# Four instead of three of eight experts on 64 places, with unsplit float32 products

## The chip, the cores and the metric

The kernel runs on one core of one Trainium2 chip. The metric is the device time of one execution, in microseconds. It is the median of several executions, lower is better.

## The reference

The program is two layers of a hybrid encoder over 256 tokens of width 1024, all in float32. Each layer has an input projection, a convolution branch, a state-space branch, an output projection and a feed-forward part. The feed-forward part of the first layer is dense. That of the second layer is a mixture of eight experts, and each token goes to two of them:

```python
def swiglu(h, w_gate, w_up, w_down):
    return (jax.nn.silu(h @ w_gate) * (h @ w_up)) @ w_down

def top2_moe(h, router_w, router_b, w_gate, w_up, w_down):
    ...
    logits = (t @ router_w + router_b).astype(jnp.float32)
    top_val, top_idx = lax.top_k(logits, TOP_K)
    top_w = jax.nn.softmax(top_val, axis=-1)
    gates = jnp.sum(jax.nn.one_hot(top_idx, N_EXPERTS, dtype=jnp.float32)
                    * top_w[..., None], axis=1)
    out = jnp.zeros((bsz * seq_len, d), jnp.float32)
    for e in range(N_EXPERTS):
        out = out + gates[:, e:e + 1] * swiglu(t, w_gate[e], w_up[e], w_down[e]).astype(jnp.float32)
```

Here D_MODEL is 1024 and D_FF is 2816, so the three weight matrices of one expert hold 33 MiB, and those of eight experts 264 MiB. A final RMS norm gives the output. With the reference's inputs the router sends 58, 53, 93, 46, 60, 38, 73 and 91 tokens to experts 0 to 7.

## The kernel before

Everything but the experts stays as it is, so only the second layer's expert part (`moe`, and `route` inside it) is told here.

**Route.** `route` ranks the tokens of each expert and sorts the experts: place 0 is always expert 0, whose weights can be asked for before the routing is known, and places 1 to 7 hold the other seven by falling token count. The first `NL` places are the big ones, the last `NS` the small ones. A big expert has 128 token places (`CAP`), a small one 64 (`CAPS`). `route` also leaves a count (`cnt`) that tells whether any expert has more tokens than places. If so, `rest` at the very end computes what did not fit, with a loop over all experts; else `rest` is skipped.

**Blocks.** An expert's hidden width is cut into 11 blocks of 256 (`NB`). A block needs two transfers of 1 MiB from `m_gu` (gate and up weights) and one from `m_down`. The transfers are issued by SyncE in the order in which the blocks use them, into a ring of eight 1 MiB buffers (`NRA` = 6 and `NRB` = 2, both named `raw`), so each transfer waits until the buffer eight transfers before it is free.

**A big block** splits the weights: for each half of a buffer ScalarE writes the rounded part `wh` and VectorE the remainder `wl` (`split`, L93 and L75). This frees the buffer. TensorE then makes three products where one is meant (high by high, high by low, low by high): 24 matmuls of 512 columns into `acc`, a silu and a product on ScalarE and VectorE (`sl`), two transposes, a split of the activations (`mah`, `mal`), and 12 matmuls of 512 columns into `py`.

**A small block** uses `raw` unsplit, in float32. The 64 places are the stationary side, so two halves of the hidden width are put on the two 64-column halves of the array: 16 matmuls into `acc` (in the trace 32 records of 256 columns), one transpose (`sls`, `mas`), and 4 matmuls into `pys` (8 records). The buffer is free when TensorE is done with it.

**Order.** The blocks stand in one list. Four big blocks come first; then the small blocks are spread evenly over the remaining big ones:

```python
        seq, n0 = big[:4], len(big) - 4
        for i, v in enumerate(big[4:]):
            seq.append(v)
            seq += few[(i * len(few)) // n0:((i + 1) * len(few)) // n0]
```

In the loop over this list the first products of a block are followed by the second products of the block before it. TensorE, VectorE and ScalarE keep the program's order. During the first blocks, side work is mixed in (`side`): the token gathers `small` (all small experts at once) and `gather1` (places 1 and 2), and, from the first block of place 1 on, `gather3` (places 3 and 4). When an expert's last block is done, `back` (big) or `back_few` (small) scatters its result into `x`, the first half at once, the second half after the next block.

Of the kernel before, what the change touches and what calls it, by code (L numbers as in the profile page):

```python
# [19 lines left out]
T = 256  # L20
# [10 lines left out]
PAD = 384  # L31
SP = mybir.EngineType.SP
NRA, NRB, NHL = 6, 2, 4
NL, NS, CAPS = 5, 3, 64
# [24 lines left out]
class Body:  # L59
# [1129 lines left out]
    def route(self):  # L1189
# [114 lines left out]
        self.dr = self.dp.tile([128, NE, 3, 2], F32, name="dr")  # L1304
        rg = sp.tile([128, NE, 3, 2], F32, name="rg")
# [63 lines left out]
    def moe(self):  # L1369
# [50 lines left out]
        def alone():  # L1420

            t = [self.gtp.tile([128, 8, 128], F32R, name="x0", tag="gate") for _ in range(2)]
            for k2 in range(4):
                for src, dst in zip((self.hth, self.htl), t):
                    ps = self.misc()
                    for k in range(2):
                        kk = 2 * k2 + k
                        for b in range(2):
                            self.mm(ps[:, k * 256:(k + 1) * 256], src[:, b, kk * 128:(kk + 1) * 128],
                                    oh[:, b, 0:1].to_broadcast([128, 2, 128]), b == 0, b == 1)  # L1430
                    nc.scalar.copy(dst[:, 2 * k2:2 * k2 + 2], ps.rearrange("p (k s) -> p k s", k=2)[:, :, 0:128])
            tok[0] = [lambda k, t=t, i=i: t[i][:, k] for i in range(2)]
# [22 lines left out]

        def gather3():
            x = [self.gtp.tile([128, 4, 2, 128], F32R, name="x3", tag="gate") for _ in range(4)]
            both([lambda k, h=h: x[2 * h + k // 4][:, k % 4] for h in range(2)], 3)
            return pair(*(lambda k2, h=h: x[2 * h + k2 // 2][:, 2 * (k2 % 2):2 * (k2 % 2) + 2]
                          .rearrange("p k e s -> p (k e s)") for h in range(2)), 3)  # L1460
# [146 lines left out]
        alone()  # L1607
# [32 lines left out]
    def rest(self):  # L1640
# [3 lines left out]
        with tc.If(n > self.cap):  # L1644
            hf = [t.bitcast(F32) for t in (self.hth, self.htl)]
            with tc.For_i(0, NE, 1) as e:
                rg = self.gp.tile([128, 3, 2], F32, name="g_r")
                nc.sync.dma_start(rg, self.dr[:, bass.ds(e, 1)].rearrange("p o i b -> p (o i) b"))
                oh = self.gp.tile([128, 2, 128], F32, name="g_oh")
                for b in range(2):  # L1650
                    nc.vector.tensor_scalar(oh[:, b], self.iota, rg[:, 0, b:b + 1], None, op0=ALU.is_equal)
                oht = self.gp.tile([128, T], F32, name="g_oht")
                gs = self.gp.tile([128, 2], F32, name="g_gs")
                ps = self.misc()
                for b in range(2):
                    self.tr(ps[:, b * 128:(b + 1) * 128], oh[:, b])
                nc.scalar.copy(oht, ps[:, :T])
                ps = self.misc()
                for b in range(2):
                    self.mm(ps[:, 0:2], oh[:, b], rg[:, 1:3, b], b == 0, b == 1)  # L1660
                nc.vector.tensor_copy(gs, ps[:, 0:2])
                xg = self.gp.tile([128, 8, 128], F32, name="g_x")
                for k in range(8):
                    ps = self.misc()
                    for j in range(4):
                        i, b = divmod(j, 2)
                        self.mm(ps[:, :128], hf[i][:, b, k * 128:(k + 1) * 128], oh[:, b], j == 0, j == 3)
                    nc.scalar.copy(xg[:, k], ps[:, :128])
                py = self.psx.tile([128, D], F32, name="py")
                for b in range(NB):  # L1670
                    pg = self.acc()
                    w = self.gp.tile([128, 2, 4, 2, 256], F32, name="g_gu")
                    for i in range(2):
                        nc.sync.dma_start(w[:, i].rearrange("p k w f -> p (k w f)"),
                                          self.a["m_gu"][bass.ds(e, 1), b, i].rearrange("o p f -> p (o f)"))
                    for j in range(2):
                        for k in range(8):
                            self.mm(pg[:, 256 * j:256 * j + 256], xg[:, k], w[:, k // 4, k % 4, j], k == 0, k == 7)
                    sl = self.gp.tile([128, 256], F32, name="g_a")
                    nc.scalar.activation(sl, pg[:, :256], AF.Silu, scale=gs[:, 1:2])  # L1680
                    self.stt(sl, pg[:, 256:], gs[:, 1:2], sl, ALU.mult, ALU.mult)
                    ps = self.misc()
                    for i in range(2):
                        self.tr(ps[:, i * 128:(i + 1) * 128], sl[:, i * 128:(i + 1) * 128])
                    at = self.gp.tile([128, 2, 128], F32, name="g_at")
                    nc.scalar.copy(at.rearrange("p k s -> p (k s)"), ps[:, :256])
                    w = self.gp.tile([128, 2, D], F32, name="g_w")
                    nc.sync.dma_start(w.rearrange("p k f -> p (k f)"),
                                      self.a["m_down"][bass.ds(e, 1), b].rearrange("o p f -> p (o f)"))
                    for k in range(2):  # L1690
                        for h in range(2):
                            s = slice(512 * h, 512 * h + 512)
                            self.mm(py[:, s], at[:, k], w[:, k, s], b == 0 and k == 0, b == NB - 1 and k == 1)
                y = self.gp.tile([128, D], F32, name="g_y")
                nc.scalar.activation(y, py, AF.Copy, scale=gs[:, 0:1])
                for d in range(8):
                    ps = self.misc()
                    self.mm(ps[:, :T], y[:, d * 128:(d + 1) * 128], oht, True, True)
                    self.add(self.x[:, d], self.x[:, d], ps[:, :T])
# [236 lines left out]
```

## Time and profile before

| What | Value |
|---|---|
| Median of 3 executions | 1428.27 us (1427.89 to 1429.31) |
| The profiled execution's own time | 1430.8 us |
| Its span, first to last instruction | 1429.0 us |
| Mean granted TensorE clock, share of 2.4 GHz | 0.972 |
| First matmul of the first expert block | 681.87 us after the span's start |
| Last weight transfer issued | 1377 us |

All later rows are from that one profiled execution. In the rows, PE is TensorE's matmul side, PEld its weight load, DVE is VectorE, ACT is ScalarE and SP is SyncE. A matmul's duration includes its latency, so matmuls overlap, and the pace is read from one start to the next.

### The profile page before, as it was taken

What the parts mean: (1) busy time and instruction counts of PE and PEld (TensorE: products, weight loads), DVE (VectorE), ACT (ScalarE), POOL (GpSimd) and SP (SyncE); (2) the same over time, 40 slices, a digit from 0 to 9 for tenths busy, and PEclk for the clock granted to TensorE, in tenths of its full rate; (3) what the DMA queues carried; (4) which work ended last, traced back from release to release, by engine and by line L of the source; (5) the groups of instructions that cost most, each with busy time, mean ns of one, the idle gap of its engine ahead of it and who ended that gap; (6) DMA issues with size and microseconds to landing.
All of it is one profiled execution on the core that took longest, in us unless ns stands there. A gap on an engine that the chain in (4) does not pass through costs nothing. (4 is left out here: it accounts for less than half of the span.)

```text
span 1429.0 us, 23540 instructions
## 1 busy us (share of the span) xinstructions
PE 1341.0 (94%) x9291; PEld 1079.3 (76%) x9291; DVE 952.3 (67%) x1413; ACT 686.1 (48%) x968; POOL 84.3 (6%) x148
## 2 busy tenths in 40 slices
PE   6989989999998969888999999999999999999995
PEld 5868879999998858886876666667676676666663
DVE  7696675788885465765775665667666666666663
ACT  3432344454444524443675555555555555555551
POOL 1052220000120040000000000000000000000000
PEclk9999999999999989998999999999999999999996
DMA  5284444566678394564689999998999999999970
GB/s 218 97 258 150 168 133 150 191 220 207 221 234 285 132 299 130 180 222 159 236 313 362 394 347 407 405 417 338 405 421 419 365 418 351 414 368 416 409 301 31
DMA packets 78307, 399.73 MB, mean 280 GB/s; under 512 B 13024, under 2 KB 15728, under 8 KB 44400
## 3 DMA queue, kind: packets, MB, share of 16 engines
q1 hardware_dynamic: 65504, 371.22, 68.0%
q0 software_dynamic: 8448, 26.31, 5.7%
q8 instruction: 75, 1.23, 0.4%
q10 hardware_dynamic: 4240, 0.64, 0.3%
q14 instruction: 40, 0.33, 0.1%
HBM read 386.51 MB, written 11.62 MB: 279 GB/s over the span
## 5 line engine op out<-in xcount | busy, mean ns | idle before, releaser
L75 DVE TENSOR_TENSOR wl<-raw,wh 128x1024 fp32r<-128x1024 f32 x460 | 549.5, 1222 | 220.5 <-ACT wh L93 220.2
L93 ACT ACTIVATE wh<-raw 128x1024 fp32r<-128x1024 f32 x460 | 470.5, 1054 | 77.1 <-issue 35.8
L116 PE MATMUL acc<-wh,x 128*128 128x512 f32 x880 | 293.9, 401 | 0.0
L116 PEld LDWEIGHTS acc<-wh,x 128*128 128x128 f32 x880 | 165.5, 188 | 44.9 <-ACT wh L93 8.9
L116 PE MATMUL acc<-wl,x 128*128 128x512 f32 x440 | 173.0, 393 | 0.0
L116 PE MATMUL acc<-hf,wh 128*128 128x256 f32 x704 | 128.4, 285 | 0.0
L116 PE MATMUL acc<-raw,xs 128*64 128x256 f32 x1056 | 127.9, 384 | 0.0
L116 PE MATMUL acc<-hh,wh 128*128 128x256 f32 x352 | 105.1, 298 | 7.0 <-ACT hh L636 3.1
L116 PE MATMUL acc<-xg,raw 128*128 128x256 f32 x448 | 103.2, 388 | 6.8 <-DMA raw<-in_w_in 6.8
L116 PEld LDWEIGHTS acc<-hf,wh 128*128 128x128 f32 x704 | 109.0, 190 | 0.2
L116 PEld LDWEIGHTS acc<-raw,xs 128*64 128x64 f32 x1056 | 71.2, 137 | 46.9 <-issue 17.5
L116 PE MATMUL acc<-hh,wl 128*128 128x256 f32 x352 | 103.0, 293 | 1.7 <-DVE wl L75 1.7
L116 PE MATMUL acc<-hl,wh 128*128 128x256 f32 x352 | 102.9, 292 | 0.0
L116 PE MATMUL acc<-hf,wl 128*128 128x256 f32 x352 | 99.9, 284 | 2.0 <-DVE wl L75 2.0
L116 PEld LDWEIGHTS acc<-xg,raw 128*128 128x128 f32 x448 | 85.8, 195 | 19.1 <-ACT xg L682 6.8
L116 PEld LDWEIGHTS acc<-wl,x 128*128 128x128 f32 x440 | 83.1, 189 | 18.0 <-DVE wl L75 1.7
L116 PE MATMUL py<-wh,mah 128*128 128x512 f32 x220 | 89.6, 407 | 0.0
L116 PE MATMUL py<-wh,mal 128*128 128x512 f32 x220 | 86.1, 391 | 0.0
L116 PE MATMUL py<-wl,mah 128*128 128x512 f32 x220 | 86.0, 391 | 0.0
L1508 ACT ACTIVATE mah<-misc 128x256 fp32r<-128x256 f32 x55 | 21.1, 384 | 128.6 <-PE misc L124 128.3
L116 PEld LDWEIGHTS acc<-hh,wh 128*128 128x128 f32 x352 | 70.7, 201 | 10.8 <-issue 4.0
L75 DVE TENSOR_TENSOR mal<-misc,mah 128x256 fp32r<-128x256 f32 x55 | 23.3, 423 | 74.9 <-ACT mah L1508 74.8
(290 smaller groups left out, 2002.6 us busy)
## 6 DMA issues: line engine op xcount, KB each, us to landing
raw<-in_m_gu SPq DMA_DIRECT2D x176, 1024.0 KB, 8.0
raw<-in_m_down SPq DMA_DIRECT2D x88, 1024.0 KB, 8.3
raw<-in_w_in SPq DMA_DIRECT2D x56, 512.0 KB, 4.1
raw<-in_f_gate SPq DMA_DIRECT2D x22, 512.0 KB, 3.5
raw<-in_f_up SPq DMA_DIRECT2D x22, 512.0 KB, 3.7
raw<-in_f_down SPq DMA_DIRECT2D x22, 512.0 KB, 3.5
raw<-in_w_out SPq DMA_DIRECT2D x16, 512.0 KB, 3.5
hs<-hc POOLq DMA_DIRECT2D x32, 142.0 KB, 5.4
```

The source lines that it names most:

```text
L75: return self.nc.vector.tensor_tensor(out, a, b, op=op)
L93: self.nc.scalar.activation(h, raw, AF.Copy)
L116: return self.nc.tensor.matmul(out, l, r, start=start, stop=stop, **kw)
L1508: nc.scalar.activation(ah, pv, AF.Copy)
```

## The change

The numbers of places change from 5 big and 3 small to 4 and 4, so the expert with the fourth-smallest count (60 tokens with these inputs) moves from 128 places and split products to 64 places and unsplit ones. `gather3` is gone; `alone`, which gathered place 0, now also gathers place 3, as a piece of side work. A padding tile goes, and two small tiles of `route` move to another pool, to make room for the larger `xs`. The general path (`rest`) reads each expert's own count and skips the expert when it fits; its body moves to a function of its own, `rest_of`, unchanged.

```diff
-PAD = 384
+PAD = 0
...
-NL, NS, CAPS = 5, 3, 64
+NL, NS, CAPS = 4, 4, 64
...
-        pm = sp.tile([128, NE, NE], F32, name="pm")
+        pm = self.c2("pm", [128, NE, NE])
...
-        t8 = sp.tile([128, NE, NE], F32, name="t8")
+        t8 = self.c2("t8", [128, NE, NE])
...
-        self.dr = self.dp.tile([128, NE, 3, 2], F32, name="dr")
-        rg = sp.tile([128, NE, 3, 2], F32, name="rg")
+        self.dr = self.dp.tile([128, NE, 4, 2], F32, name="dr")
+        rg = sp.tile([128, NE, 4, 2], F32, name="rg")
...
+        self.add(few, few, ps[:, 16:24])
+        nc.vector.tensor_copy(rg[:, :, 3], few[:, :, None].to_broadcast([128, NE, 2]))
         nc.gpsimd.dma_start(self.dr, rg)
-        self.add(few, few, ps[:, 16:24])
...
-        def alone():
+        def alone(j):
...
+            tok[j] = [lambda k, i=i: t[i][:, k] for i in range(2)]
...
-                                    oh[:, b, 0:1].to_broadcast([128, 2, 128]), b == 0, b == 1)
+                                    oh[:, b, j:j + 1].to_broadcast([128, 2, 128]), b == 0, b == 1)
...
-        def gather3():
-            x = [self.gtp.tile([128, 4, 2, 128], F32R, name="x3", tag="gate") for _ in range(4)]
...
-        alone()
+        for _ in alone(0):
+            pass
...
                 if v == (1, 0):
-                    side.append(gather3())
+                    side.append(alone(3))
...
+                ne = self.gp.tile([1, 1], I32, name="g_n")
+                nc.vector.tensor_copy(ne, rg[0:1, 3, 0:1])
+                with tc.If(nc.values_load(ne[0:1, 0:1]) > self.cap):
+                    self.rest_of(e, rg, hf)
```

The instruction order shows what the list of blocks becomes. On ScalarE, in the middle of the expert part, a big block shows as an `sl` and a `mah` among its `wh` splits, a small one as an `sls` and a `mas`. Before, a stretch reads:

```order
L1492 ACTIVATE sls<-acc,gs_7641 128x128
L93 ACTIVATE wh<-raw 128x1024 x2
L1501 COPY mas<-misc 128x128
L93 ACTIVATE wh<-raw 128x1024 x3
L1492 ACTIVATE sl<-acc,gs_8180 128x256
L93 ACTIVATE wh<-raw 128x1024
L1508 ACTIVATE mah<-misc 128x256
L93 ACTIVATE wh<-raw 128x1024 x3
L1492 ACTIVATE sl<-acc,gs_8180 128x256
```

After the change a stretch of the same engine and part reads:

```order
L1488 ACTIVATE sls<-acc,gs_7643 128x128
L93 ACTIVATE wh<-raw 128x1024 x2
L1497 COPY mas<-misc 128x128
L93 ACTIVATE wh<-raw 128x1024
L1488 ACTIVATE sl<-acc,gs_8139 128x256
L93 ACTIVATE wh<-raw 128x1024
L1504 ACTIVATE mah<-misc 128x256
L93 ACTIVATE wh<-raw 128x1024 x2
L1488 ACTIVATE sls<-acc,gs_7643 128x128
```

Before, a small block (`sls`) is followed by one or by two big blocks (`sl`); after, a big block is always followed by a small one. In counts: of the blocks behind the first four, 51 big and 33 small become 40 big and 44 small. Before, each of the 33 small blocks stands alone between big ones, and 18 big blocks follow another big one. After, there are 40 pairs of a big and a small block and, four times, a second small block.

On TensorE, a small block before always stands behind a big one (`py` of the big block after the second `acc<-raw,xs`):

```order
L116 MATMUL pys<-raw,mas 64x512 x4
L116 MATMUL acc<-raw,xs 64x256 x8
L124 MATMUL misc<-ident,sl 128x128 x2
L116 MATMUL acc<-raw,xs 64x256 x8
L116 MATMUL py<-wh,mah 128x512
```

At one of the four places where two small blocks now stand together, TensorE's order is:

```order
L116 MATMUL py<-wh,mal 128x512
L116 MATMUL acc<-raw,xs 64x256 x8
L124 MATMUL misc<-ident,sls 128x128
L116 MATMUL acc<-raw,xs 64x256 x8
L116 MATMUL pys<-raw,mas 64x512 x4
L116 MATMUL acc<-wh,x_7383 128x512
```

The second small block has the transpose of a small block (`sls`) between its halves, and `pys` behind it instead of twelve `py`.

## Rows read from the trace of the kernel before

**Rows 1.** The page: busy time of TensorE; clock and bandwidth in 40 slices

```profile
PE 1341.0 (94%) x9291; PEld 1079.3 (76%) x9291; DVE 952.3 (67%) x1413; ACT 686.1 (48%) x968; POOL 84.3 (6%) x148
...
PEclk9999999999999989998999999999999999999996
...
GB/s 218 97 258 150 168 133 150 191 220 207 221 234 285 132 299 130 180 222 159 236 313 362 394 347 407 405 417 338 405 421 419 365 418 351 414 368 416 409 301 31
```

**Rows 2.** Stretches of the expert part: length, busy time, granted clock, DMA share, GB/s

```profile
682.00:740.00 58.00, 57.73 (x279) 48.25 (x278) 42.34 (x58) 39.30 (x54) 0.57 (x1) 1.00 0.73 275
...
1000.00:1100.00 100.00, 100.00 (x517) 68.88 (x517) 65.36 (x71) 56.04 (x76) 0.00 (x0) 1.00 1.01 414
1100.00:1120.00 20.00, 18.08 (x101) 13.55 (x102) 13.08 (x16) 10.56 (x14) 0.00 (x0) 1.00 0.92 368
...
1400.00:1429.00 29.00, 15.86 (x68) 11.63 (x64) 9.33 (x26) 3.62 (x7) 0.00 (x0) 0.62 0.12 38
```

**Rows 3.** Waits of TensorE, 681.8 to 1392 us: total, times, longest

```profile
PE misc L116 <- ACT oht L1550: 5.3, 6, 1.2
PE misc L116 <- DVE yl L87: 2.0, 3, 0.7
```

**Rows 4.** Timeline of TensorE, 1033 to 1071 us: start, duration

```profile
1033.30 1.95 PE L116 MATMUL acc<-raw,xs 128*64 128x256 f32 x16
1035.18 0.44 PE L124 MATMUL misc<-ident,sl 128*128 128x128 f32 x2
1035.55 1.95 PE L116 MATMUL acc<-raw,xs 128*64 128x256 f32 x16
1037.42 0.50 PE L116 MATMUL py<-wh,mah 128*128 128x512 f32 x1
...
1045.95 1.94 PE L116 MATMUL pys<-raw,mas 128*64 128x512 f32 x8
1047.72 1.90 PE L116 MATMUL acc<-raw,xs 128*64 128x256 f32 x16
...
1070.89 1.95 PE L116 MATMUL acc<-raw,xs 128*64 128x256 f32 x16
```

**Rows 5.** Timeline of TensorE, 687 us: two of 16 such rows

```profile
687.50 0.51 PE L116 MATMUL misc<-oh,hth 128*128 128x384 f32 x2
687.85 0.51 PE L116 MATMUL misc<-oh,htl 128*128 128x384 f32 x2
```

**Rows 6.** Timeline of TensorE where a small and a big expert end

```profile
956.24 0.44 PE L124 MATMUL misc<-ident,oh 128*128 128x128 f32 x2
...
959.27 0.51 PE L116 MATMUL acc<-wh,x 128*128 128x512 f32 x1
...
1108.48 0.38 PE L124 MATMUL misc<-ident,oh 128*128 128x128 f32 x2
...
1112.20 1.95 PE L116 MATMUL acc<-raw,xs 128*64 128x256 f32 x16
```

**Rows 7.** Timeline of TensorE at the end

```profile
1399.16 3.42 PE L116 MATMUL pys<-raw,mas 128*64 128x512 f32 x8 [0.35 <-ACT mas L1501]
1402.51 0.59 PE L124 MATMUL misc<-ident,oh 128*128 128x128 f32 x2
...
1411.69 6.95 PE L116 MATMUL misc<-ones,sq 128*128 128x1 f32 x32 [3.43 <-PEq L1644]
```

**Rows 8.** The page: expert weight transfers, median us from issue to landing

```profile
raw<-in_m_gu SPq DMA_DIRECT2D x176, 1024.0 KB, 8.0
raw<-in_m_down SPq DMA_DIRECT2D x88, 1024.0 KB, 8.3
```

**Rows 9.** The fastest ten microseconds seen, columns as in rows 2

```profile
1140.00:1150.00 10.00, 10.00 (x45) 6.82 (x44) 7.19 (x9) 6.07 (x8) 0.00 (x0) 1.00 1.01 426
```

**Rows 10.** The page: the splits of weights, mean ns of one

```profile
L75 DVE TENSOR_TENSOR wl<-raw,wh 128x1024 fp32r<-128x1024 f32 x460 | 549.5, 1222 | 220.5 <-ACT wh L93 220.2
L93 ACT ACTIVATE wh<-raw 128x1024 fp32r<-128x1024 f32 x460 | 470.5, 1054 | 77.1 <-issue 35.8
```

More of the change, by code (lines that the diff above doesn't have):

```diff
@@ L1429, in alone @@
                             self.mm(ps[:, k * 256:(k + 1) * 256], src[:, b, kk * 128:(kk + 1) * 128],
-                                    oh[:, b, 0:1].to_broadcast([128, 2, 128]), b == 0, b == 1)
+                                    oh[:, b, j:j + 1].to_broadcast([128, 2, 128]), b == 0, b == 1)
                     nc.scalar.copy(dst[:, 2 * k2:2 * k2 + 2], ps.rearrange("p (k s) -> p k s", k=2)[:, :, 0:128])
-            tok[0] = [lambda k, t=t, i=i: t[i][:, k] for i in range(2)]
+                    yield
         def small():
@@ L1646, in rest @@
             with tc.For_i(0, NE, 1) as e:
-                rg = self.gp.tile([128, 3, 2], F32, name="g_r")
+                rg = self.gp.tile([128, 4, 2], F32, name="g_r")
                 nc.sync.dma_start(rg, self.dr[:, bass.ds(e, 1)].rearrange("p o i b -> p (o i) b"))
[L1649 to L1662, printed above, removed]
@@ L1663, in rest @@
-                for k in range(8):
[L1664 to L1699, printed above, removed]
+                ne = self.gp.tile([1, 1], I32, name="g_n")
+                nc.vector.tensor_copy(ne, rg[0:1, 3, 0:1])
+                with tc.If(nc.values_load(ne[0:1, 0:1]) > self.cap):
+                    self.rest_of(e, rg, hf)
@@ new lines, in rest_of @@
+    def rest_of(self, e, rg, hf):
+        nc = self.nc
+        oh = self.gp.tile([128, 2, 128], F32, name="g_oh")
+        for b in range(2):
+            nc.vector.tensor_scalar(oh[:, b], self.iota, rg[:, 0, b:b + 1], None, op0=ALU.is_equal)
+        oht = self.gp.tile([128, T], F32, name="g_oht")
+        gs = self.gp.tile([128, 2], F32, name="g_gs")
+        ps = self.misc()
+        for b in range(2):
+            self.tr(ps[:, b * 128:(b + 1) * 128], oh[:, b])
+        nc.scalar.copy(oht, ps[:, :T])
+        ps = self.misc()
+        for b in range(2):
+            self.mm(ps[:, 0:2], oh[:, b], rg[:, 1:3, b], b == 0, b == 1)
+        nc.vector.tensor_copy(gs, ps[:, 0:2])
+        xg = self.gp.tile([128, 8, 128], F32, name="g_x")
+        for k in range(8):
+            ps = self.misc()
+            for j in range(4):
+                i, b = divmod(j, 2)
+                self.mm(ps[:, :128], hf[i][:, b, k * 128:(k + 1) * 128], oh[:, b], j == 0, j == 3)
+            nc.scalar.copy(xg[:, k], ps[:, :128])
+        py = self.psx.tile([128, D], F32, name="py")
+        for b in range(NB):
+            pg = self.acc()
+            w = self.gp.tile([128, 2, 4, 2, 256], F32, name="g_gu")
+            for i in range(2):
+                nc.sync.dma_start(w[:, i].rearrange("p k w f -> p (k w f)"),
+                                  self.a["m_gu"][bass.ds(e, 1), b, i].rearrange("o p f -> p (o f)"))
+            for j in range(2):
+                for k in range(8):
+                    self.mm(pg[:, 256 * j:256 * j + 256], xg[:, k], w[:, k // 4, k % 4, j], k == 0, k == 7)
+            sl = self.gp.tile([128, 256], F32, name="g_a")
+            nc.scalar.activation(sl, pg[:, :256], AF.Silu, scale=gs[:, 1:2])
+            self.stt(sl, pg[:, 256:], gs[:, 1:2], sl, ALU.mult, ALU.mult)
+            ps = self.misc()
+            for i in range(2):
+                self.tr(ps[:, i * 128:(i + 1) * 128], sl[:, i * 128:(i + 1) * 128])
+            at = self.gp.tile([128, 2, 128], F32, name="g_at")
+            nc.scalar.copy(at.rearrange("p k s -> p (k s)"), ps[:, :256])
+            w = self.gp.tile([128, 2, D], F32, name="g_w")
+            nc.sync.dma_start(w.rearrange("p k f -> p (k f)"),
+                              self.a["m_down"][bass.ds(e, 1), b].rearrange("o p f -> p (o f)"))
+            for k in range(2):
+                for h in range(2):
+                    s = slice(512 * h, 512 * h + 512)
+                    self.mm(py[:, s], at[:, k], w[:, k, s], b == 0 and k == 0, b == NB - 1 and k == 1)
+        y = self.gp.tile([128, D], F32, name="g_y")
+        nc.scalar.activation(y, py, AF.Copy, scale=gs[:, 0:1])
+        for d in range(8):
+            ps = self.misc()
+            self.mm(ps[:, :T], y[:, d * 128:(d + 1) * 128], oht, True, True)
+            self.add(self.x[:, d], self.x[:, d], ps[:, :T])
```

3 lines of the change are left out of this document (removed).

## The prediction

> **What bounds the kernel now.** I first read the page: TensorE is busy 94% of the span, and in the second half the transfers run near 400 GB/s [rows 1]. So two things can bound the expert part, TensorE and the weight transfers, and busy shares alone don't choose between them. The stretches come next. From 1000 to 1100 us TensorE is busy all the time at the full granted clock (2.4 GHz), while the transfers move 414 GB/s at a DMA share of 1.01 [rows 2]. The reader is to see that both look full. The waits decide: in the 710 us from 681.8 to 1392 the two longest kinds of wait of TensorE sum to 7.3 us, and both are waits for a finished expert's result (`oht`, `yl`), none for a weight [rows 3]. TensorE bounds the expert part, with the transfers close behind. So the change is priced by TensorE's time per block, and then I ask whether the transfers can follow.
>
> **The blocks.** TensorE's timeline gives the pace from start to start [rows 4]. From the small block at 1033.30 to the next at 1047.72 lie one small and one big block: 14.42 us. From 1047.72 to 1070.89 lie one small and two big ones: 23.17 us, so a big block behind a big one costs 8.75 us. No row shows a small block behind a small one. I build it from its parts: 1.88 us (1033.30 to 1035.18), 1.87 us (1035.55 to 1037.42), 1.77 us for `pys` (1045.95 to 1047.72), and at most the 0.37 us that the two transposes take between 1035.18 and 1035.55. That is 5.9 us at the most and 5.5 us without the transpose; I take 5.9 us, since the array changes its mode there too.
>
> Behind the first four blocks, before: 33 pairs and 18 further big blocks, 33 × 14.42 + 18 × 8.75 = 475.9 + 157.5 = 633.4 us. After: 40 pairs and four further small blocks, 40 × 14.42 + 4 × 5.9 = 576.8 + 23.6 = 600.4 us. **Saved: 33.0 us.** The four first blocks stay as they are.
>
> A rule of the Trainium skill speaks against this step. "FP8 and Floating Point Precision", TensorE Precision Notes, says that true float32 takes four passes through the array, where the split product takes three matmuls. By that alone an unsplit product would be the dearer one. The trace weighs against the rule here: two halves of 64 columns share the array, and the first product of a small block takes 3.75 us [rows 4], of the 14.42 us of a pair. By the row the step saves 33.0 us; by four passes without that sharing it would lose about 25 us (last rival).
>
> **The other terms on TensorE.**
> - The gather `small` has 32 matmuls that grow from 384 to 512 columns. Two of them take 0.35 us now [rows 5], 0.174 us each; in proportion 0.231 us, so +0.058 × 32 = **+1.9 us**. They stand between the first blocks, where TensorE doesn't wait, so they count in full.
> - `alone(3)` in place of `gather3`: both write 256 columns per matmul in eight steps of four matmuls. 0.
> - Expert ends: one `back` becomes one `back_few`. The first half of a small one takes 3.03 us (956.24 to 959.27), of a big one 3.72 us (1108.48 to 1112.20) [rows 6]. The second half of the small one is likely dearer, as it reads float32. I take **0**, with 1 us either way.
> - The end: the last `pys` takes 3.42 us [rows 7] against 1.94 us in the middle [rows 4], because the granted clock falls, to 0.62 on average over the last 29 us [rows 2]; that is between the two levels of 1.2 and 2.4 GHz. Before the change, a big expert ends one block before the last, and its waits lie just ahead of that `pys`. After it, two small blocks follow the last big one. So the clock likely holds a block longer. I take **-1.5 us**, between 0 and -2.5 (the 1.5 us of `pys`, and 1 us more if what follows it gains too).
>
> **What costs nothing, and what hides it.** VectorE loses 66 splits of 1.22 us and ScalarE as many of 1.05 us [rows 10]; neither is waited for, so this gives nothing. If the splits were what TensorE waits for, it would be up to 80 us; rows 3 exclude it. `route` gets one more small VectorE copy and an addition earlier; later splits queue behind them on VectorE, for 0.3 us at most, while TensorE works at the first block. SyncE issues the same 264 transfers of 1 MiB. The new branch stands inside the skipped loop.
>
> **Can the transfers follow?** A pair needs six transfers. At 426 GB/s, the most seen in ten microseconds [rows 9], one takes 1.0486 MB / 426 GB/s = 2.46 us, six take 14.77 us. TensorE will want them in 14.42 us. So the transfers fall behind by 0.35 us a pair, and by 7.4 - 5.9 = 1.5 us at a further small block. Within a round of ten pairs and one further small block that is 5.0 us. Two things cover it. First, in each round one big and one small expert end, and TensorE takes no weights for 3.7 and 3.0 us in the first halves alone [rows 6]; the ring fills meanwhile. Second, the ring: now 15 transfers pass in 37.59 us (1033.30 to 1070.89), so a buffer comes round after 8 × 2.51 = 20.0 us. Of these 8.0 us are from issue to landing [rows 8], so data lies there for some 12 us before its buffer is free. The least it needs is 1.05 + 2 × 1.22 = 3.5 us for both halves of a big one [rows 10], and 1.9 us for a small one. Some 8 us are spare, more than the 5.0 us of a round. I take **0**. With no cover at all, the lag would count in full: 40 × 0.35 + 4 × 1.5 = 20 us. These are the two ends.
>
> **The sum.** -33.0 + 1.9 + 0 - 1.5 + 0 = -32.6 us. The profiled span of 1429.0 us becomes 1396.4 us, and its own time of 1430.8 us (1.8 us lie around the span) becomes 1398.2 us. The median is 2.5 us below that execution's time, so I expect a median of about 1396 us.
>
> **The rivals.**
> - *The transfers become the bound.* For it: 414 GB/s now against 426 GB/s at best [rows 2, 9], and the new pace asks for 6.29 MB / 14.42 us = 436 GB/s. Against it: the 8 us of spare time in the ring and the pauses at expert ends. If the whole lag shows: 1396 + 20 = 1416 us. Half of it gives 1406 us. The Trainium skill's "HBM Reference", Specifications, puts a core's share at about 358 GB/s and says under the same heading that a core that streams alone measures about 425 GB/s. Rows 9 agree with the second; by the first, six transfers would take 17.6 us and the kernel would be far slower already than the 14.42 us a pair that is measured. 14%.
> - *No change.* If the transfers had been the bound all along, TensorE's savings would turn into waits: 1428 us. The 414 GB/s speak for it, TensorE's waits [rows 3] against it. 4%.
> - *Slower: the general path.* If one of the four small experts had over 64 tokens, `rest` would run at the end, with nothing beside it. It loads 33 MiB for that expert into single buffers: at 2.46 us per MiB at least 81 us, so 1477 us or more. It decides from the 65th token on; the inputs give 60, 53, 46 and 38 for the four. 2%.
> - *Slower: unsplit float32 is dearer than it looks.* If the two halves of 64 columns did not share the array, a small block would cost twice its 5.5 us, 11 us, and each of the 11 swapped blocks would lose 2.3 us: about +25 us, 1453 us. Rows 4 show the pair at 14.42 us with such a block in it. The rule of four passes, above, is the page's side of this. 1%.
>
> **How the numbers follow.** My forecast has 78%. Its own range is 1389 to 1404 us: downward, small blocks of 5.5 us (-1.6), expert ends 1 us cheaper, the end at -2.5 us (-1.0) and 3 us for stretches that I did not add up one by one; upward, 1.5 us at the end, 1 us at the expert ends and one round's lag of 5.0 us. The range given reaches past half the lag, to 1410 us, and down to 1388 us. A difference of 0.2% (2.9 us) is about what can be told from no change here. Faster by more: the forecast and the first rival, 0.92. Within 0.2%: the second rival, 0.04. Slower: the last two rivals and the hundredth that no case names, 0.04.
>
> **What would show each step.** In the profile after, small and big blocks should alternate at 14.4 us a pair, with TensorE busy without gaps and the transfers at 420 GB/s or more between expert ends. A small block behind a small one should take 5.5 to 5.9 us. The expert part should hold 264 splits on ScalarE instead of 330. The matmuls of the final norm, which start at 1411.69 us now [rows 7], should start near 1379 us. I am wrong if TensorE's `acc` rows wait for a DMA or for `wh` towards the end of each round, if the granted clock falls within the expert part, or if `g_` tiles show up at the end.

## The result, and the profile after

The changed kernel takes 1403.57 us (median of 4, 1401.46 to 1404.89) beside 1428.79 us for the kernel before (4 executions on the same chip, 1427.89 to 1430.28): ratio 0.9821, 95% interval 0.9804 to 0.9838, a gain of 25.2 us. The forecast was 1396 us and a gain of 32.6 us. The sign, the cause and the range hold; 7.4 us of the gain are missing, and most of the experiments went after them.

The profiled execution took 1404.2 us, with a span of 1402.1 us. The page after, against [rows 1, 8]: busy times, GB/s in 40 slices, and the expert weight transfers with their median time from issue to landing.

```profile
PE 1315.7 (94%) x9324; PEld 1038.9 (74%) x9324; DVE 872.6 (62%) x1336; ACT 618.7 (44%) x902; POOL 84.4 (6%) x148
...
GB/s 223 94 263 150 179 121 166 182 212 220 211 232 299 126 271 164 201 137 244 179 264 381 407 419 372 401 382 420 421 391 401 421 420 420 414 388 420 420 332 31
...
raw<-in_m_gu SPq DMA_DIRECT2D x176, 1024.0 KB, 8.8
raw<-in_m_down SPq DMA_DIRECT2D x88, 1024.0 KB, 9.2
```

TensorE lost 25.3 us of busy time, ScalarE 67.4 us and VectorE 79.7 us; only the first of these is what the time shows. The bandwidth rose as expected, and a transfer lands 0.8 to 0.9 us later. Whether that costs anything is asked of TensorE's waits, over the stretch of [rows 3]:

```profile
PE misc L116 <- ACT oht L1546: 7.7, 8, 1.2
PE misc L116 <- PEq L1641: 3.4, 1, 3.4
PE misc L116 <- DVE yl L87: 2.7, 4, 0.7
```

Again there is no wait for a weight. (The second row is the branch around `rest`, ahead of the final norm, which stood outside this stretch before.) The stretch of [rows 3] ends ahead of the last two expert ends of the kernel before. Up to 1409 us, its waits for the one-hot rows of a finished expert are:

```profile
PE misc L116 <- ACT oht L1550: 6.5, 7, 1.2
```

So these waits grew from 6.5 us in seven to 7.7 us in eight. Those for `yl` are 2.7 us in four in both kernels.

The timeline of TensorE after shows the pace of a pair, and, in the first four rows, the new case of a small block behind a small one, against [rows 4]:

```profile
1043.53 1.95 PE L116 MATMUL acc<-raw,xs 128*64 128x256 f32 x16
1045.41 0.33 PE L124 MATMUL misc<-ident,sls 128*128 128x128 f32 x1
1045.66 1.95 PE L116 MATMUL acc<-raw,xs 128*64 128x256 f32 x16
1047.44 1.89 PE L116 MATMUL pys<-raw,mas 128*64 128x512 f32 x8
...
1295.15 1.90 PE L116 MATMUL acc<-raw,xs 128*64 128x256 f32 x16
...
1309.66 1.90 PE L116 MATMUL acc<-raw,xs 128*64 128x256 f32 x16
```

From 1295.15 to 1309.66 is a pair: 14.51 us, where the forecast had 14.42. It is one of the longer ones: of the pairs without a gather or an expert's end in them, 17 take 14.37 to 14.44 us, and eight, all from 1237 us on, 14.50 or 14.51. The small block's own parts in the upper rows are 1.88, 0.25 and 1.78 us up to `pys`, and 1.82 us for that, up to the next row at 1049.26: 5.7 us, within the 5.5 to 5.9 that were built from parts.

The gather `small`, against [rows 5], takes 0.46 us from this row to the next, for two matmuls, where it took 0.35:

```profile
684.79 0.62 PE L116 MATMUL misc<-oh,hth 128*128 128x512 f32 x2
```

The last view is TensorE's timeline at the end of the second big expert, against [rows 6]. The granted clock of the 7 us around it stands in the row of the stretches behind it (columns as in [rows 2]), and the end of the expert part, against [rows 7], below that:

```profile
1008.17 0.38 PE L124 MATMUL misc<-ident,oh 128*128 128x128 f32 x2
1009.79 0.39 PE L116 MATMUL misc<-oht,yh 128*128 128x256 f32 x1 [1.25 <-ACT oht L1546]
1010.85 0.38 PE L116 MATMUL misc<-oht,yl 128*128 128x256 f32 x1 [0.67 <-DVE yl L87]
...
1011.95 0.63 PE L116 MATMUL acc<-wh,x 128*128 128x512 f32 x1
1012.38 0.63 PE L116 MATMUL acc<-wl,x 128*128 128x512 f32 x1
...
1015.08 0.39 PE L116 MATMUL acc<-wl,x 128*128 128x512 f32 x1
...
1364.32 3.03 PE L116 MATMUL acc<-raw,xs 128*64 128x256 f32 x16
...
1373.39 1.94 PE L116 MATMUL pys<-raw,mas 128*64 128x512 f32 x8 [0.41 <-ACT mas L1497]
...
1383.70 7.22 PE L116 MATMUL misc<-ones,sq 128*128 128x1 f32 x32 [3.42 <-PEq L1641]
```

```profile
1009.00:1016.00 7.00, 5.53 (x20) 4.43 (x21) 3.78 (x4) 2.74 (x5) 0.00 (x0) 0.76 1.02 420
1361.00:1368.00 7.00, 5.59 (x29) 3.51 (x31) 2.66 (x3) 0.95 (x3) 0.00 (x0) 0.76 0.01 4
```

TensorE pauses 1.25 and 0.67 us; then matmuls of 512 columns follow each other by 0.43 us instead of 0.23 (1011.95 to 1012.38), until 1015: the granted clock has fallen to its lower level, 1.2 GHz (0.50 from 1012 to 1014 us). The same happens at 1364.32, where a row that takes 1.95 us elsewhere takes 3.03. The last `pys` runs at full speed now, 1.94 us instead of 3.42. The matmuls of the final norm start at 1383.70 us, 28.0 us earlier; 2.7 us of these lie ahead of the expert part, whose first matmul starts at 679.16 us instead of 681.87.

So the expert part, from its first matmul to the final norm, took 729.82 us and takes 704.53: -25.3 us. To see where they are, I summed the distances from one start to the next over TensorE's rows, by kind of row:

| us in the expert part | before | after | change | forecast |
|---|---|---|---|---|
| products of big blocks (`acc`, `py`) and their transposes | 485.0 | 394.3 | | |
| products of small blocks (`acc`, `pys`) and theirs | 186.6 | 246.4 | | |
| all blocks | 671.6 | 640.7 | -30.9 | -34.5 |
| gathers | 14.6 | 16.8 | +2.1 | +1.9 |
| expert ends: one-hot transposes and waits | 9.4 | 11.0 | +1.6 | |
| expert ends: scatter | 31.0 | 32.9 | +1.8 | |
| expert ends together | 40.4 | 43.9 | +3.4 | 0 |

Each number is rounded by itself; what is left to the whole, 3.2 us in both, are rows on `gr`. The forecast of -34.5 is -33.0 for the blocks and -1.5 for the clock at the end. Behind the expert part, the final norm takes 18.45 us instead of 17.34: +1.1 us.

### The profile page after: what moved, and what is told of

Read it like the earlier page. It is cut to its first block, busy times and chain, and to the rows that moved or that the text cites. A ratio compares the mean times of both kernels' runs of the same rounds, so it can differ in the third digit from the quotient of the medians.

```text
span 1402.1 us, 23377 instructions
## 1 busy us (share of the span) xinstructions
PE 1315.7 (94%) x9324; PEld 1038.9 (74%) x9324; DVE 872.6 (62%) x1336; ACT 618.7 (44%) x902; POOL 84.4 (6%) x148
## 5 line engine op out<-in xcount | busy, mean ns | idle before, releaser
L75 DVE TENSOR_TENSOR wl<-raw,wh 128x1024 fp32r<-128x1024 f32 x394 | 474.1, 1221 | 235.1 <-ACT wh L93 234.8
L93 ACT ACTIVATE wh<-raw 128x1024 fp32r<-128x1024 f32 x394 | 407.7, 1054 | 76.2 <-issue 35.1
L116 PE MATMUL acc<-wh,x 128*128 128x512 f32 x704 | 234.1, 401 | 0.0
L116 PE MATMUL acc<-raw,xs 128*64 128x256 f32 x1408 | 171.0, 385 | 0.0
L116 PEld LDWEIGHTS acc<-wh,x 128*128 128x128 f32 x704 | 132.9, 189 | 33.5 <-ACT wh L93 1.6
L116 PEld LDWEIGHTS acc<-raw,xs 128*64 128x64 f32 x1408 | 96.4, 137 | 65.3 <-issue 25.8
L116 PE MATMUL acc<-wl,x 128*128 128x512 f32 x352 | 138.3, 393 | 0.0
L116 PE MATMUL pys<-raw,mas 128*64 128x512 f32 x352 | 85.0, 604 | 0.4 <-ACT mas L1497 0.4
L87 DVE SCALAR_TENSOR_TENSOR sl<-acc,gs,sl 128x256 f32<-128x256 f32 x44 | 21.2, 483 | 85.0 <-ACT sl L1488 85.0
L116 PEld LDWEIGHTS acc<-hh,wl 128*128 128x128 f32 x352 | 69.6, 198 | 2.3 <-DVE wl L75 2.3
```

Of the source, the lines that this page charges most:

```text
L75: return self.nc.vector.tensor_tensor(out, a, b, op=op)
L87: return self.nc.vector.scalar_tensor_tensor(out, a, s, b, op0=op0, op1=op1)
L93: self.nc.scalar.activation(h, raw, AF.Copy)
L116: return self.nc.tensor.matmul(out, l, r, start=start, stop=stop, **kw)
```

## The experiments

All but one stand on the kernel after or before with a few lines changed. Each ratio is to executions of the kernel before that stood beside the run.

**1. The rest of the change alone.** Five big and three small experts as before, with everything else of the change:

```diff
-NL, NS, CAPS = 4, 4, 64
+NL, NS, CAPS = 5, 3, 64
...
-                    side.append(alone(3))
+                    side += [alone(3), alone(4)]
```

> The changed kernel with its numbers put back to 5 big and 3 small places; everything else of the change stays (the general path, the pools, no padding tile, places 3 and 4 gathered by alone). Theory A (TensorE sets the pace, and the whole gain comes from the 11 blocks that became small): within 3 us of the kernel before, about 1429 us. Rival B (the transfers set a good part of the pace, and gathers or buffers moved them): a part of the 25 us remains, 1405 to 1422 us.

Measured: 1437.8 us, ratio 1.0068 (1.0042 to 1.0095). The gain is gone, so it comes with the fourth small expert, and nothing else in the change makes the kernel faster. It is 7.8 us slower than the kernel before, more than the 3 us of theory A. In good part that is the edit's own: places 3 and 4 are now gathered one by one, and the gathers take 19.1 us on TensorE instead of 14.6. What makes the other 3 us was not followed.

**2. and 3. The ends one block later.** What an expert's end costs, taken from the kernel after and from the kernel before: the first half of the scatter is issued one block behind the transposes and not straight behind them, so that the one-hot rows and `yl` are there when TensorE comes to them. The lines are the same in both:

```diff
-        def more():
-            while extra:
+        def more(n):
+            for _ in range(n):
...
+            old = len(extra)
...
-            more()
+            more(old)
...
-            more()
+            more(1)
```

> The changed kernel, with the first half of an expert's scatter put one block later, so that TensorE no longer waits for the scaled result and the turned one-hot. Theory A: the shortfall against the forecast (25 us instead of 32.6) sits mostly at the expert ends; the waits after the change sum to 7.7 + 2.7 us there, and all but the last expert's vanish: 8 to 10 us less, 1394 to 1396 us. Rival B: the transfers lag and would only be waited for instead: within 3 us of 1403.6 us.

> The same edit on the kernel before. Theory A: its waits at expert ends sum to 5.3 + 2.0 us up to 1392 us, so 5 to 7 us less, 1422 to 1424 us; the distance to the changed kernel with the same edit is then 27 to 29 us. Rival B: no change, 1428 us.

Measured: 1392.03 us (ratio 0.9743, 0.9721 to 0.9765), and for the kernel before 1417.55 us (0.9925, 0.9904 to 0.9946). TensorE's timeline at the same big expert's end, and its longest waits to 1380 us, both of the kernel after with deferred ends (2.):

```profile
1004.85 0.38 PE L124 MATMUL misc<-ident,oh 128*128 128x128 f32 x2
1004.99 0.48 PE L116 MATMUL acc<-wh,x 128*128 128x512 f32 x1
...
1013.28 0.39 PE L116 MATMUL misc<-oht,yh 128*128 128x256 f32 x1
```

```profile
PE misc L116 <- PEq L1642: 3.8, 1, 3.8
...
PE acc L116 <- DVE wl L75: 1.0, 3, 0.4
```

The block goes on 0.14 us behind the transposes, of the waits for `oht` one of 0.2 us is left and of those for `yl` none, and the granted clock stays at its full level up to 1368 us. The transposes with their waits cost 1.8 us instead of 11.0, the scatter of big experts 10.3 instead of 14.0. So putting the ends off is worth 11.5 us to the kernel after, a little more than the 8 to 10 us of theory A. But the kernel before gains as much: 12.5 us against the 1430.03 us beside it, twice the 5 to 7 us of theory A. (The waits added up there stop at 1392 us and leave out the 1.9 us behind the last big expert; what makes the rest was not followed.) So the distance between the two kernels stays at 25.5 us, under the expected 27 to 29. By rows of one profile each, the distance of the expert parts is 28.2 us here and 25.3 us without the edit; the medians, whose executions spread over 5.6 and 8.1 us, don't show these 2.9 us. The blocks alone differ by 31.8 us in this pair of profiles, in which the blocks of neither kernel meet a fall of the clock.

**4. Less work for TensorE.** In the second product of big blocks, the matmuls of the low part of the activations are left out, a third of 126 us:

```diff
-                    self.mm(py[j][:, s], ah[:, k], wl[:, s], False, False)
-                    self.mm(py[j][:, s], al[:, k], wh[:, s], False, stop)
+                    self.mm(py[j][:, s], ah[:, k], wl[:, s], False, stop)
```

> The changed kernel without the low-by-high product of the second matmuls of big blocks; the output loses that part. It takes 44 x 4 matmuls of 0.228 us, 40 us, off TensorE and leaves every transfer as it is. If nothing but TensorE mattered: 1363 us. Theory A (TensorE bounds the changed kernel, transfers close behind): the transfers take over on the way. From 742 us on, 239 transfers at 2.47 us end at 1332 us, and some 38 us of last blocks, scatter and norm follow: 1368 to 1378 us. Rival B (the transfers bound the changed kernel already): over 1393 us.

Measured: 1386.72 us (ratio 0.9687, 0.9651 to 0.9722), between the two ranges. A row of ScalarE's waits from 1000 to 1350 us, and a stretch without an expert's end, with the columns of [rows 2], first of this run and then of the kernel after, and TensorE's longest wait in this run's stretch:

```profile
ACT wh L93 <- DMA raw<-in_m_down: 31.6, 10, 4.8
```

```profile
1100.00:1160.00 60.00, 57.03 (x304) 35.68 (x304) 32.95 (x37) 29.88 (x42) 0.00 (x0) 1.00 1.01 421
1100.00:1160.00 60.00, 60.00 (x328) 40.51 (x327) 34.20 (x37) 29.53 (x41) 0.00 (x0) 1.00 1.01 421
```

```profile
PE py L116 <- DVE wl L75: 2.1, 6, 0.5
```

This is how the bound by transfers announces itself: the splits on ScalarE wait for data, 31.6 us in all, and TensorE waits for splits in a stretch in which, at the same 421 GB/s, the kernel after is busy all 60 us. In the kernel after, ScalarE's list from 1000 to 1350 us has no wait for a transfer. So of 42 us of work that TensorE is spared, 17 us come out, and waits for transfers are part of what eats the rest. More falls of the clock are another part: the unchanged `acc` rows of big blocks take 7.5 us more, and the mean granted clock of the profile is 0.959 against 0.970. What each takes wasn't parted.

**5. and 6. Half the bytes.** The straight test of the first rival: every expert weight transfer moves half of its MiB, and the products read that half twice.

```diff
-            ins = self.nc.sync.dma_start(raw, src)
+            ins = self.nc.sync.dma_start(raw[:, :1024], src[:, :1024])
...
-                    yield self.split(raw[:, 1024 * h:1024 * h + 1024], 1024)
+                    yield self.split(raw[:, :1024], 1024)
...
-                                    xs[:, kk, j - NL], w[:, k, :, h], kk == 0, kk == 7)
+                                    xs[:, kk, j - NL], w[:, k % 2, :, h], kk == 0, kk == 7)
...
-                                w[:, 1024 * k + 512 * h:1024 * k + 512 * h + 512], b == 0 and k == 0, last and k == 1)
+                                w[:, 512 * h:512 * h + 512], b == 0 and k == 0, last and k == 1)
```

> The kernel after, with half of each expert weight transfer (0.5 MiB of each MiB) left out; the split products and the unsplit ones read the loaded half twice, so the instructions on TensorE, ScalarE and VectorE are the same in number and shape, and the output is not the reference's. Theory A (the transfers cost the change nothing; its missing 7 us lie on TensorE itself, in expert ends and granted clock): within 2.5 us of the kernel after, so 1401 to 1406 us. Theory B (full transfers hold TensorE back by what is missing): 1394 to 1398 us.

> The kernel before with the same halved transfers. Theory A: within 2.5 us of the kernel before, and 24 to 27 us above the kernel after with halved transfers. Theory B: the kernel before has transfers to spare, so it too stays within 2.5 us, but the distance grows to 30 to 34 us.

Measured: 1404.37 us (ratio 0.9846, 0.9828 to 0.9864) and 1427.87 us (0.9997, 0.9981 to 1.0012), 23.5 us apart, half a microsecond under theory A's 24 to 27 us and far from theory B's 30 to 34. Two stretches of the kernel after with halved transfers, the first stretch again in the full kernel after, and TensorE's waits with halved transfers as above:

```profile
1000.00:1100.00 100.00, 97.40 (x532) 64.64 (x529) 54.70 (x63) 44.38 (x64) 0.00 (x0) 0.98 0.60 200
1100.00:1160.00 60.00, 60.00 (x329) 39.87 (x329) 33.38 (x37) 29.57 (x42) 0.00 (x0) 1.00 0.66 217
...
1000.00:1100.00 100.00, 97.40 (x536) 63.82 (x533) 55.09 (x63) 44.51 (x66) 0.00 (x0) 0.98 1.00 404
```

```profile
PE misc L116 <- ACT oht L1546: 7.7, 8, 1.2
...
PE misc L116 <- DVE yl L87: 2.7, 4, 0.7
```

At half the bandwidth TensorE's 97.40 us of busy time in 100, its granted clock of 0.98 and its waits are those of the full kernel (the last row of the stretches, at 404 GB/s), and the expert part takes 704.26 us against 704.53. The transfers cost the kernel after nothing, for all their DMA share of 1.01. Theory A holds, B falls.

**7. and 8. One buffer fewer.** Seven buffers of 1 MiB, in the kernel after and in the one with deferred ends (2.):

```diff
-NRA, NRB, NHL = 6, 2, 4
+NRA, NRB, NHL = 5, 2, 4
```

> The kernel after with seven instead of eight buffers of 1 MiB for the weights. Theory A (the cover is nearly used up: at the end of a round a weight is there only 0.9 to 1.5 us before its use, and one buffer less takes some 2.4 us from that): 1 to 1.5 us of waiting in each of four rounds, 4 to 6 us slower than the kernel after, 1407 to 1410 us. Theory B (some 8 us are spare in the ring, as the prediction had it): within 2 us of the kernel after, 1402 to 1406 us.

> The kernel after with the first half of a finished expert's scatter one block later, which took 1392 us with eight buffers, now with seven. Theory A (as above, and here TensorE pauses less at expert ends, so that the ring has less time to fill): 5 to 10 us slower, 1397 to 1402 us. Theory B: within 2 us, 1390 to 1394 us.

Measured: 1403.28 us (ratio 0.9823, 0.9804 to 0.9843) and 1391.92 us (0.9753, 0.9732 to 0.9774): no change in either. Here theory A falls, which was mine by then. The short leads at the end of a round were read as cover that is nearly spent. They may be what is left at the worst place of a ring that fills again at each expert end; no row shows this by itself. The prediction's 8 us of spare time stand this test better.

**9. The halves apart.** What makes a small block cheap: in its first product the halves of 64 columns stand four and four and don't alternate.

```diff
-                    for k in range(4):
-                        kk = 4 * i + k
-                        for h in range(2):
+                    for h in range(2):
+                        for k in range(4):
+                            kk = 4 * i + k
```

> The kernel after; in the first product of a small block the two halves of 64 columns no longer alternate from matmul to matmul: four matmuls of the one half stand together, then four of the other. The same 16 matmuls and the same sums. Theory A (two unsplit float32 matmuls on different halves run beside each other, and that is why the small block is cheap): the first product takes up to twice its 3.75 us, less what neighbours at the changes of half still share; 44 blocks by 2.3 to 3.75 us are 100 to 165 us, so 1500 to 1570 us. Theory B (the order of the halves plays no part, an unsplit matmul simply takes some 0.23 us): 1402 to 1406 us.

Measured: 1485.96 us (ratio 1.0397, 1.0358 to 1.0436). The first half of a first product on TensorE's timeline, from 1059.69 to the transposes:

```profile
1059.69 2.86 PE L116 MATMUL acc<-raw,xs 128*64 128x256 f32 x16
1062.49 0.44 PE L124 MATMUL misc<-ident,sl 128*128 128x128 f32 x2
```

A half takes 2.80 us instead of 1.88, and 44 blocks by 2 × 0.92 are 81 us of the 82.4 us that the kernel lost. The order alone does it: neighbours on different halves run beside each other, and groups of four share less. It is less than the 100 us of theory A, whose range began at 1500 us; that matmuls at each change of half still share some is likely, but no row shows it by itself. By this difference, the fourth small expert would have been worth 11 × 1.84 = 20 us less in a kernel written that way (an estimate). The Trainium skill's "TensorEngine Tiling (Array Packing)", Key Properties, says that different tiles of the array can work in parallel. The run agrees, and shows that how much of it one gets depends on the order in the program: 1.88 us against 2.80.

**10. The wait filled.** Idle matmuls in the waits at expert ends, to part the wait from the fall of the clock behind it:

```diff
+        def fill(n):
+            ps = self.misc()
+            for _ in range(n):
+                self.mm(ps, self.hth[:, 0, 0:128], self.hth[:, 0, 0:512], True, True)
...
             o = oht(j, F32R)
             yield
+            fill(5)
...
             o = oht(j, F32)
             yield
+            fill(3)
```

> The kernel after with matmuls that nobody reads laid into TensorE's wait for the one-hot rows at every expert end: five of 512 columns (some 0.22 us each) at a big expert's end, three at a small one's. No wait is moved or shortened; the wait is only filled. Theory A (TensorE's pause at an expert end, with the thin work around it, is what lets the granted clock fall just behind the end): the two stretches of half clock inside the expert part, at about 1011 and 1364 us, go away, and 2 to 3 us with them: 1400.5 to 1402 us, and the matmuls of the final norm start 1.5 to 3 us earlier behind the first block. Theory B (the clock falls for another reason, such as the unsplit products): the stretches stay, and the time is 1403 to 1405 us.

Measured: 1400.5 us (ratio 0.9802, 0.9777 to 0.9827), which the interval alone would not tell from the kernel after. That is at the lower edge of theory A's 1400.5 to 1402 us. The same end as in the kernel after, and the same two stretches:

```profile
1008.38 0.38 PE L124 MATMUL misc<-ident,oh 128*128 128x128 f32 x2
1008.51 1.41 PE L116 MATMUL misc<-hth 128*128 128x512 f32 x5
1010.07 0.35 PE L116 MATMUL misc<-oht,yh 128*128 128x256 f32 x1
1011.06 0.39 PE L116 MATMUL misc<-oht,yl 128*128 128x256 f32 x1 [0.64 <-DVE yl L87]
...
1012.00 0.40 PE L116 MATMUL acc<-wh,x 128*128 128x512 f32 x1
1012.24 0.40 PE L116 MATMUL acc<-wl,x 128*128 128x512 f32 x1
```

```profile
1009.00:1016.00 7.00, 6.21 (x30) 4.78 (x30) 4.74 (x5) 3.14 (x5) 0.00 (x0) 1.00 1.02 422
1361.00:1368.00 7.00, 6.36 (x47) 3.73 (x48) 2.35 (x4) 0.63 (x2) 0.00 (x0) 1.00 0.01 2
```

The scatter starts no earlier behind its transposes (1.7 us, and 1.6 in the kernel after), yet the clock is 1.00 where it was 0.76, the matmuls behind it follow by 0.24 us, and the expert part is 2.5 us shorter (702.01 us). So the clock falls there only with the pause, and theory B is out: the unsplit products alone, which are all still there, don't make it fall. That one profile without a fall is no accident: the profiles after and of runs 5, 7 and 11, with the same program on TensorE in the blocks, all show a fall behind the second and behind the fourth big expert. But the pause alone is not enough either. Behind the first and the third big expert, at 828 and 1184 us, TensorE waits the same 1.25 and 0.67 us, and in none of these four profiles does the clock fall there. The third big expert's end in the kernel after:

```profile
1183.00:1190.00 7.00, 5.08 (x27) 3.92 (x26) 5.40 (x7) 2.83 (x6) 0.00 (x0) 1.00 1.01 421
```

What sets the ends with a fall apart from those without stays open.

**11. and 12. The general path.** Its bound is lowered, so that one expert counts as too large:

```diff
-    def __init__(self, tc, a, out, dbg=None, cap=CAP):
+    def __init__(self, tc, a, out, dbg=None, cap=123):
```

(116 in the kernel before.)

> The kernel after with the bound of the general path set to 123 in place of 128, as the counts enter it (a small expert's 64 is added): of the eight experts only the one with 60 tokens is above it (124), so the path runs for it alone, with no token in its places, which adds zeros to the result. Theory A (as in the third rival: 33 transfers of 1 MiB into single buffers, with nothing beside them): at least 81 us, and more for the matmuls that wait for each of them and for eight looks at a count: 1490 to 1600 us. Theory B (the path is cheap, since its loads stream as in the expert part and the work on them is small): below 1485 us.

> The kernel before with the bound set to 116: one expert above it (124) sends all eight through the path, with no token in their places. Theory A (the look at each expert's own count is worth seven of eight passes through the path): 8 times what one expert costs in the run beside this one, so 2080 to 3000 us. Theory B (one pass through the path costs most, the later ones stream behind it): below 1900 us.

Measured: 1609.16 us (ratio 1.1267, 1.1212 to 1.1321), above the 1490 to 1600 us of theory A, and 2724.67 us (1.9077, 1.8996 to 1.9158), inside its 2080 to 3000. In the kernel before eight passes cost 1296.8 us (beside 1427.86), 162 us each. In the kernel after, one pass and eight looks at a count cost 205.6 us (against the 1403.57 us above); with the 162 us of the kernel before for the pass, a look costs some 5.4 us (an estimate). TensorE's timeline of one block of the path, in the kernel after:

```profile
1462.03 1.89 PE L116 MATMUL acc<-g_gu,g_x 128*128 128x256 f32 x8
1465.04 5.45 PE L116 MATMUL acc<-g_gu,g_x 128*128 128x256 f32 x24 [1.13 <-DMA g_gu<-in_m_gu]
...
1472.53 3.70 PE L116 MATMUL py<-g_w,g_at 128*128 128x512 f32 x8 [0.52 <-ACT g_at L1690]
1476.07 2.36 PE L116 MATMUL acc<-g_gu,g_x 128*128 128x256 f32 x9
```

A block takes 14.04 us (1462.03 to 1476.07), of which the one wait for a weight is 1.13 us; the block from 1488.97 us on has no such wait and takes 12.89 us. The path is bound by unsplit products over the full width, one after the other, and not by its loads.

## Why the prediction was right, and where its sizes were off

**What bounds the kernel** was read rightly: TensorE. Halving the bytes changes neither kernel (5, 6), and undoing the fourth small expert undoes the gain (1).

**The blocks** were forecast at -33.0 us. In the profiles they give -30.9 us, in which the last `pys` has -1.5 us of clock and the two falls behind expert ends +2.3 us (1.2 us in six `acc` matmuls at 1012 us, which take 2.56 us from start to start instead of 1.38, and 1.1 us at 1364 us); without these, -31.7 us. In the pair with deferred ends they give -31.8 us. So this term was right to some 4%. The pair chosen for it was a fair one: of ten undisturbed pairs in the kernel before, five take 14.42 us and five 14.50 or 14.51, and 17 of 25 after are within 0.05 us of 14.42. The other eight take 14.50 or 14.51, and pairs with a gather or an end in them have 14.5 to 14.8 us in their own rows; the 1.3 us that are missing were not followed further.

**The gather** was +1.9 us by proportion of the columns, and is +2.1.

**The expert ends** were taken at 0, with 1 us either way, and came to +3.4 us. This step failed in size. It compared the first halves of a small and a big end [rows 6] and overlooked which ends stood next to each other. Before, a big expert ends 11.65 us behind a small one (956.24 and 967.89 us), and the last small one 8.12 us behind a big one (1394.39 and 1402.51 us). At the second end of each, the second half of the earlier expert's scatter stands right behind the transposes, so TensorE has work while the new one-hot rows are made (at 967.89 the new scatter begins only a block later, at 977.56 us):

```profile
967.89 0.38 PE L124 MATMUL misc<-ident,oh 128*128 128x128 f32 x2
968.20 1.13 PE L116 MATMUL misc<-oht,ys 64*128 64x256 f32 x4
```

From the transposes to the next row are 0.31 us here and 0.35 us at 1402.51, against 1.1 us at the other small ends and 1.6 us at the other big ones. After the change no end is covered by another, and all eight waits show: +1.6 us. The rest, +1.8 us, is the scatter. The prediction named the dearer second half of a small expert but gave it no price: over both halves, in the kernel before, a small expert's scatter takes 5.2 us and a big one's 3.1, waits included. Part of it also ran at the lower clock after the change.

**The end and the clock** were taken at -1.5 us. The mechanism named there came in part: the last `pys` takes 1.94 us again. But the fall behind the last big expert is not gone. It comes earlier, on the first small block behind that end (+1.1 us at 1364 us), and another fall stands behind the second big expert (+1.2 us). Together the clock gives +0.8 us instead of -1.5. A fall within the expert part was one of the prediction's own signs of being wrong; here it cost 2.3 us and left the other steps standing. That there is no fall without the pause of the expert end was shown by filling it (10). It is less sure that this counts against the change itself: the profile of the kernel before with halved transfers, whose TensorE program is that of the kernel before, shows two such falls, where the profile of the kernel before has none.

```profile
955.00:960.00 5.00, 5.00 (x17) 3.76 (x16) 2.88 (x4) 0.78 (x2) 0.00 (x0) 0.66 0.33 116
1109.00:1114.00 5.00, 4.68 (x25) 3.05 (x25) 2.77 (x4) 0.16 (x1) 0.00 (x0) 0.66 0.00 2
```

**The final norm** was no term of the sum and takes 1.1 us more. Its matmuls run at the lower clock level in both kernels. From their start to VectorE's last row are 10.50 and 10.76 us, and from there to the span's end, while the output is written, 6.8 and 7.7 us. So most of it is not the clock.

**The sum.** Against the forecast the profiles miss 3.4 us for the ends, 2.3 for the clock, 1.3 for the blocks, 1.1 for the norm and 0.2 for the gather: 8.3 us. The layers ahead were 2.7 us shorter in the profiled execution, and the time around the span 0.3 us longer, so its own time missed its forecast of 1398.2 us by 6.0 us; the medians miss by 7.6. No single cause holds the shortfall, and what the medians add to it beyond these terms stays open.

**The transfers** were taken at 0, between 0 and 20 us, and that was right (5, 7, 8). The worry that a pair needs 14.77 us of transfers and gets 14.42 was half right: the cover holds the lag, and where TensorE is spared another 42 us of work it no longer does in full (4).

**The rivals.** The bound by transfers and the lack of any change are excluded by 5 and 6. That unsplit float32 is dear without the shared array was rightly priced in direction: alternation in the first product alone is worth 82 us to the kernel after (9). The Trainium skill's "FP8 and Floating Point Precision", TensorE Precision Notes, has four passes for true float32, and where nothing is shared the trace nearly agrees. In the general path a product over the full width is two records of some 0.23 us for 256 columns (24 records from 1465.04 on take 5.45 us), and one of 512 columns takes 0.89 us (four from 1472.53 to 1476.07), against 0.23 us for a split one: nearly four times as long. It doesn't decide here because the shared halves take nearly half of that back (0.24 us a product of 256 columns instead of some 0.45). The general path was priced at 81 us or more from its loads; it costs 206 us, since its own products bind it and not the loads. The bound was true, and far from the cost.

**A better version** came out of 2.: the kernel after with deferred ends, 1392.03 us, and 1391.92 us again with seven buffers.

## What to carry to other kernels

A stage whose transfers run at the most that the chip was seen to move need not be bound by them: halve the bytes and look whether the time moves, before a full DMA share or short leads are taken for a bound. An expert's end, or any step at which TensorE waits for its own result by way of another engine, costs more than its wait, since the clock can fall behind it; issue such a step one block later. When work is reordered, count which of these waits were hidden by a neighbour, because the reorder can uncover them.

## What the runs showed of the hardware

- A pause of TensorE of 1.25 and 0.67 us was followed by three to four microseconds at the lower clock level behind two of four big experts, in four profiles of four, and by no fall behind the other two. Matmuls that nobody reads, laid into the pause, kept the level up: 0.76 against 1.00 over the same 7 us.
- Two unsplit float32 products on different halves of 64 columns run beside each other if they are neighbours in the program: 1.88 us for eight that alternate, 2.80 us for eight in groups of four.
- The expert part's first matmul started between 674.41 us (the kernel before with deferred ends) and 683.83 us (run 4) over the fourteen profiles, with nearly the same program ahead of it. This spread of 9.4 us sits in the layers ahead, and it is part of the spread of the executions from which the medians are taken.
